# FoX attention moved beside the Strassen pairs of the input projection, with a ring of three weight parts

## The chip, the core and the metric

The kernel runs on one core of a Trainium2 chip. It is one launch for a whole decoder layer. The metric is the device time in microseconds (us), the median of the runs. Engines are named as in the profile: PE (TensorE) multiplies, PEld is its weight load, DVE (VectorE), ACT (ScalarE) and POOL (GpSimd) do the elementwise work, and SP issues DMAs.

## What is computed

One layer for 1024 prompt tokens and 8 x 4 sample tokens together (1056 columns). An input projection feeds three token mixers, GLA, FoX and HGRN2. Their outputs are gated, merged and projected; a SwiGLU block follows.

```python
z = rms_norm(x) @ w_in          # gq gk gv glr gr fq fk fv ff hq hf hi hg ga gb gc
o_a, o_c = gated_linear_scan(...), gated_linear_scan(...)     # GLA and HGRN2, 4 heads each
# FoX on the prompt, 4 heads of 128, in blocks of 128 queries:
c = cumsum(log_sigmoid(ff + bias))
s = q_block @ k.T / sqrt(128) + c[query] - c[key]             # keys up to the query
o_b = softmax(s) @ v
merged = sigmoid(ga) * (o_a @ wa) + sigmoid(gb) * (o_b @ wb) + sigmoid(gc) * (o_c @ wc)
h = x + merged @ w_out
y = rms_norm(h + swiglu(rms_norm(h)))
```

The sample's FoX reads a paged past as well.

## The kernel before

Activations lie as [128 features, 1056 tokens]. For the projections every fp32 operand is split in a rounded part (h) and a rest (l); three products of these stand for one. The rounding is an ACT copy and the rest a DVE subtraction (`split`, L214 and L215).

The stages, in the order of the program:

- **Start** (`norm1` and two jobs): the norm, and the tiles fq 0, fk 0, fv 0 and fq 1 of the projection.
- **Pairs** (`in_pairs`, `pair_run`): 44 more tiles in 22 pairs. A pair is one level of Strassen's scheme: seven products (P1 to P7), each of two column groups of 12 matmuls of 264 columns, 168 matmuls in all. Four banks of PSUM hold the chains X and Z, one or two hold Y; evictions (L1700 on DVE, L1702 on ACT) read a chain while later products go on adding to it. The weights come as two raw tiles of 512 KB (`pair_load`, L1623). Four sums of them (`pair_sums`, L1630 to L1634) and seven splits (`pair_split`) make the seven parts of a pair, which lie in a ring of four tiles of two parts. After product 3 and later ones of a pair the parts of the next are made; the load after next is asked for behind product 6. `post` multiplies a pair by the norm (L568: one tile on DVE, one on POOL), for the gates gr, hq and hg also by their sigmoid (L572, L574), and stores it in `z_dram` (L602).
- **Mixers** (`phase_m`, then `mixer_jobs` and the first jobs of `out_jobs`): 16 gate tiles as plain jobs (L136, 72 matmuls of 352 columns each) and the first branch jobs. Beside them run generators in queues: `bg` with the four heads of FoX on the prompt, `bg3` with two GLA pairs and four HGRN heads, `bgs` with their sample parts, `bg2` with the sample's FoX (started from head 2). `pump` takes one step of each queue, twice per column chunk of a job.
- **Outputs, feed-forward up and down**: the rest of the branch jobs and the output projection, 22 Strassen pairs (`ffn_up`), plain jobs and 8 Strassen pairs with 126 matmuls (`down_pairs`). All pair stages share `pair_run`.

The framework orders each engine's instructions at build time, by program order as priority and by when its own cost estimates call an instruction ready. So PE's order in the trace is near to the program's but not the same. On the chip each engine takes its queue in turn.

`fox_head` (L723) fetches v, q and k and the log-forget row of its head, turns v token-major (L707), sums the row (L1146), and for each of eight query blocks makes the scores in fp32 (L780), subtracts and takes the maximum (L784, and L789 on the diagonal), Exp (L798), normalises (L797, L799, L800), turns the block by four transposes to a bank (L746, copied by L748) and multiplies by v (L759). A block's turning comes two blocks later (DEPTH).

Of the kernel before, what the change touches and what calls it, by code (L numbers as in the profile page):

```python
# [18 lines left out]
NP = 1024  # L19
# [38 lines left out]
PAIRS += [(n, t) for n, c in (("gq", 2), ("gk", 2), ("gv", 4), ("gr", 4), ("hq", 4), ("hf", 4), ("hg", 4), ("hi", 4)) for t in range(c)]  # L58
# [32 lines left out]
class Body:  # L91
# [179 lines left out]
    def run(self):  # L271
# [21 lines left out]
        self.st = [pe.tile([128, 512], F32, name=f"st{i}") for i in range(3)]  # L293
# [5 lines left out]
    def all_jobs(self):  # L299
# [7 lines left out]
        yield Job(None, 0, None, None, run=self.in_pairs, ahead=lambda: self.pair_ahead(lambda n: self.A["winp"][n], len(PAIRS) // 2))  # L307
# [4 lines left out]
    def phase_m(self):  # L312
# [15 lines left out]
        self.bg += [self.fox_head(h) for h in range(4) if ("fv", h) not in TILES[4:]]  # L328
# [221 lines left out]
    def in_pairs(self, job, nxt):  # L550
# [4 lines left out]
        def phase():  # L555
            self.close("s")
            p = self.open("p", "right", reuse_waits="tile")
            self.u = Slots(p, 6, [128, NT], F32, "pu")
            return [(p.tile([128, 1024], F32R, name=f"rh{i}"), p.tile([128, 1024], F32R, name=f"rl{i}")) for i in range(2)]

        def post(n, y):
# [7 lines left out]
            if name in ("gr", "hq", "hg"):  # L569
                g = [self.u.get(), self.u.get()]  # L570
                for i in range(2):
                    self.sig = nc.scalar.activation(g[i], y[i], AF.Sigmoid)  # L572
                for i in range(2):
                    e[i].tensor_tensor(y[i], y[i], g[i], ALU.mult)  # L574
                self.u.put(*g)
            for i in range(2):
                self.keep(*PAIRS[2 * n + i], y[i])
            self.u.put(*y)
# [15 lines left out]
        self.pair_run(nxt, phase, post, hook)  # L594
# [38 lines left out]
    def mixer_jobs(self):  # L633
        for n, h in TILES[4:]:
            yield self.store(n, h, (lambda h=h: self.bg.append(self.fox_head(h))) if n == "fv" else None)
# [85 lines left out]

    def fox_head(self, h):
        nc = self.nc  # L723
        yield from self.room(5)
        vT, q, k = [self.fetch(n, h) for n in ("fv", "fq", "fk")]
        cb = self.u.get()
        nc.sync.dma_start(cb, self.lf_dram[h:h + 1, :].to_broadcast([128, NT]))
        yield
        v, vu = self.tok_major(vT, None)
        self.u.put(vT)  # L730

        self.sums(cb, NP)
        yield
        if h == SAMPLE_WITH:
            self.bg2.append(self.fox_sample())
        yield from self.room(4)
        o = self.u.get()
        psos = {}

        def turned(i, x):  # L740

            for j0 in range(0, i + 1, 4):
                nb = min(4, i + 1 - j0)
                pt = self.pm.get()
                for j in range(nb):
                    nc.tensor.transpose(pt[:, j * 128:(j + 1) * 128], x[:, (j0 + j) * 128:(j0 + j + 1) * 128], self.ident)  # L746
                P = self.hf.get()
                nc.scalar.activation(P[:, :nb * 128], pt[:, :nb * 128], AF.Copy)  # L748
                self.pm.put(pt)
                if j0 + nb == i + 1:  # L750
                    self.u.put(x)
                yield j0, nb, P

        def values(i, j0, nb, P):
            if i % 4 == 0 and j0 == 0:
                psos[0] = self.pm.get()
            pso = psos[0]
            for j in range(nb):
                nc.tensor.matmul(pso[:, (i % 4) * 128:(i % 4 + 1) * 128], v[:, j0 + j, :], P[:, j * 128:(j + 1) * 128],  # L759
                                 start=j0 + j == 0, stop=j0 + j == i)  # L760
            self.hf.put(P)
            if i % 4 == 3 and j0 + nb == i + 1:
                nc.vector.tensor_copy(o[:, (i - 3) * 128:(i + 1) * 128], pso)
                self.pm.put(pso)

        prev = []
        for i in range(8):
            n = (i + 1) * 128
            x = self.u.get()
            cbd = self.sp.tile([128, 128], F32, tag="cbd", name="cbd", bufs=2)  # L770
            nc.gpsimd.tensor_tensor(cbd, cb[:, n - 128:n], self.cmask, ALU.add)
            m = self.sp.tile([128, 4], F32, tag="fm", name="fm", bufs=4)
            init = -3.0e38
            nm = 0
            tp = turned(*prev.pop(0)) if len(prev) == DEPTH else iter(())
            for s0 in range(0, n, 512):
                part = next(tp, None)
                w = min(512, n - s0)
                ps = self.pm.get()
                nc.tensor.matmul(ps[:, :w], q[:, i * 128:(i + 1) * 128], k[:, s0:s0 + w], start=True, stop=True)  # L780
# [13 lines left out]
                if part:  # L794
                    values(i - DEPTH, *part)
            sm = self.sp.tile([128, 4], F32, tag="fs", name="fs", bufs=4)
# [4 lines left out]
            prev.append((i, x))  # L801
            yield
        for i, x in prev:
            for part in list(turned(i, x)):
                values(i, *part)
            if i < 7:
                yield
        nc.sync.dma_start(self.o_dram[4 + h][:, 0:NP], o[:, 0:NP])
        self.u.put(q, k, vu, cb, o)

    def fox_sample(self):
# [1275 lines left out]
```

## Time and profile before

| what | us |
|---|---|
| median of 3 runs | 1998.83 (1998.76 to 2003.77) |
| the profiled execution | 2003.84 |
| its span in the profile | 2002.0 |
| PE busy | 1936.3 |
| DVE busy | 1372.3 |
| ACT busy | 808.6 |
| POOL busy | 456.6 |

The stages lie in the span like this: start to 75, pairs to 534, mixers to about 1090, outputs to 1262, feed-forward up to 1733, down and the end to 2002. Busy time is the time in which an engine had an instruction in flight. The granted clock is the share of PE's full clock; the two levels are 2.4 and 1.2 GHz, so 0.94 over a stretch means that part of it ran at the lower one.

### The profile page before, as it was taken

What the parts mean: (1) busy time and instruction counts of PE and PEld (TensorE: products, weight loads), DVE (VectorE), ACT (ScalarE), POOL (GpSimd) and SP (SyncE); (2) the same over time, 40 slices, a digit from 0 to 9 for tenths busy, and PEclk for the clock granted to TensorE, in tenths of its full rate; (3) what the DMA queues carried; (4) which work ended last, traced back from release to release, by engine and by line L of the source; (5) the groups of instructions that cost most, each with busy time, mean ns of one, the idle gap of its engine ahead of it and who ended that gap; (6) DMA issues with size and microseconds to landing.
All of it is one profiled execution on the core that took longest, in us unless ns stands there. A gap on an engine that the chain in (4) does not pass through costs nothing. (4 is left out here: it accounts for less than half of the span.)

```text
span 2002.0 us, 36377 instructions
## 1 busy us (share of the span) xinstructions
PE 1936.3 (97%) x14590; PEld 1816.3 (91%) x14590; DVE 1372.3 (69%) x2279; ACT 808.6 (40%) x1448; POOL 456.6 (23%) x269
## 2 busy tenths in 40 slices
PE   8899999999989999999999999999999999999997
PEld 6899999999976777787788999999999999999996
DVE  8866577666476767667744555878777777667965
ACT  5433343333244435355343333543333333323435
POOL 5110122211121322112201631133222322111004
PEclk9999999999988989999999999999999999999999
DMA  3343222333434226676775443221222122333212
GB/s 132 108 158 132 99 106 97 107 107 119 135 139 152 96 98 217 213 225 220 231 252 198 160 156 119 75 75 67 101 80 75 65 83 75 133 113 121 84 59 87
DMA packets 88630, 253.65 MB, mean 127 GB/s; under 512 B 13634, under 2 KB 18690, under 8 KB 88450
## 3 DMA queue, kind: packets, MB, share of 16 engines
q1 hardware_dynamic: 86898, 250.02, 36.8%
q8 instruction: 117, 1.92, 0.4%
q10 hardware_dynamic: 1296, 0.67, 0.1%
q14 instruction: 63, 0.52, 0.1%
q0 software_dynamic: 256, 0.52, 0.1%
HBM read 183.80 MB, written 67.37 MB: 125 GB/s over the span
## 5 line engine op out<-in xcount | busy, mean ns | idle before, releaser
L136 PE MATMUL pg<-x,wh 128*128 128x352 f32 x1692 | 434.0, 336 | 11.5 <-DVE ub L629 6.7
L136 PEld LDWEIGHTS pg<-x,wh 128*128 128x128 f32 x1692 | 298.1, 192 | 37.0 <-issue 26.2
L1693 PE MATMUL pg<-x,wh 128*128 128x264 f32 x1632 | 308.6, 285 | 3.4 <-DVE du L1700 2.3
L136 PE MATMUL pg<-x,wl 128*128 128x352 f32 x846 | 280.6, 332 | 0.1
L1693 PE MATMUL pg<-x,rh 128*128 128x264 f32 x1424 | 267.3, 285 | 2.2 <-DVE fu L1700 2.2
L1693 PEld LDWEIGHTS pg<-x,wh 128*128 128x128 f32 x1632 | 253.3, 188 | 5.7 <-DVE du L1700 2.5
L1693 PE MATMUL pg<-x,wl 128*128 128x264 f32 x816 | 231.7, 284 | 2.3 <-DVE wl L215 2.3
L1693 PEld LDWEIGHTS pg<-x,rh 128*128 128x128 f32 x1424 | 221.7, 189 | 2.5 <-DVE fu L1700 2.4
L1693 PE MATMUL pg<-x,rl 128*128 128x264 f32 x712 | 202.8, 285 | 0.0
L136 PEld LDWEIGHTS pg<-x,wl 128*128 128x128 f32 x846 | 162.4, 192 | 4.2 <-issue 3.0
L1693 PEld LDWEIGHTS pg<-x,wl 128*128 128x128 f32 x816 | 153.4, 188 | 2.5 <-DVE wl L215 2.5
L568 POOL TENSOR_TENSOR pu<-pu,r 128x1056 f32<-128x1056 f32 x21 | 59.2, 2818 | 378.6 <-ACT pu L1702 378.6
L1693 PEld LDWEIGHTS pg<-x,rl 128*128 128x128 f32 x712 | 134.6, 189 | 0.0
L214 ACT ACTIVATE wh<-wf 128x512 fp32r<-128x512 f32 (+2 forms) x110 | 68.1, 619 | 158.9 <-PE pg L1693 120.2
L215 DVE TENSOR_TENSOR wl<-wf,wh 128x512 fp32r<-128x512 f32 (+2 forms) x110 | 85.6, 778 | 46.7 <-ACT wh L214 45.2
L1728 POOL TENSOR_TENSOR fu<-fu,r 128x1056 f32<-128x1056 f32 x22 | 67.2, 3057 | 215.9 <-ACT fu L1702 202.7
L107 ACT ACTIVATE wh<-wf 128x1024 fp32r<-128x1024 f32 (+2 forms) x60 | 51.3, 854 | 146.8 <-PE pg L136 105.8
L1630 DVE TENSOR_TENSOR st<-wf 128x512 f32<-128x512 f32 x44 | 87.2, 1982 | 32.8 <-DMA wf<-in_winp 19.0
L1693 PE MATMUL pg<-pr,wh 128*128 128x264 f32 x544 | 103.1, 288 | 3.7 <-ACT pu L1702 3.7
L1700 DVE TENSOR_TENSOR pu<-pu,pg 128x264 f32<-128x264 f32 x132 | 56.4, 428 | 72.2 <-PE pg L1693 71.9
L215 DVE TENSOR_TENSOR rl<-wf,rh 128x512 fp32r<-128x512 f32 x85 | 69.8, 822 | 47.7 <-ACT rh L214 46.8
L214 ACT ACTIVATE rh<-wf 128x512 fp32r<-128x512 f32 x85 | 53.5, 631 | 112.2 <-PE pg L1693 83.7
(519 smaller groups left out, 4594.6 us busy)
## 6 DMA issues: line engine op xcount, KB each, us to landing
z_dram<-pu SPq DMA_DIRECT2D x44, 528.0 KB
wf<-in_winp SPq DMA_DIRECT2D x44, 512.0 KB
wf<-in_wgu SPq DMA_DIRECT2D x44, 512.0 KB
u<-z_dram SPq DMA_DIRECT2D x36, 528.0 KB
ub<-z_dram SPq DMA_DIRECT2D x28, 528.0 KB
wf<-in_win SPq DMA_DIRECT2D x19, 512.0 KB
a_dram<-fu SPq DMA_DIRECT2D x18, 528.0 KB
du<-a_dram SPq DMA_DIRECT2D x14, 528.0 KB
```

Source lines behind the costliest of these rows:

```text
L107: nc.scalar.activation(wh[:, :n], wf[:, :n], AF.Copy)
L136: nc.tensor.matmul(ps[:m, :CW], a[:, k, :], b[:, sl], start=n == 0, stop=n == 3 * job.kt - 1)
L214: nc.scalar.activation(h, x, AF.Copy)
L215: (eng or nc.vector).tensor_tensor(l, x, h.bitcast(F32), ALU.subtract)
L568: e[i].tensor_tensor(y[i], y[i], self.r1, ALU.mult)
L1630: nc.vector.tensor_tensor(s[0], a2[:, x], a2[:, y], ALU.add)
L1693: nc.tensor.matmul(ps, a[:, w], b, start=first and m == 0, stop=m == 3 * K - 1, skip_group_check=not first)
L1700: nc.vector.tensor_tensor(out, out, ps, ALU.add)
L1728: TT = lambda e, o, x, y, op=ALU.mult: e.tensor_tensor(o, x, y, op)
```

## The change

- The prompt's FoX leaves the mixer stage. Its four heads run in `bg` during the pair stage. `pair_run` gets a function `beside`, called after every column group, and `in_pairs` pumps `bg` there; what is left is drained behind the pairs.
- `fox_head` is rewritten in smaller steps with tiles of its own (`fox_open`): one score bank, one bank of transposes, or one value block per step. Query blocks are fetched and outputs stored one by one. The copy of an output leaves DVE for ACT. A block's turning comes one block later.
- To make room, the ring of the input pairs has three tiles instead of four, the pair stage has five buffers instead of six, and the sums of weights share one buffer and are made in place. The pairs get six PSUM banks instead of seven, FoX two.
- The order of sums, splits and loads changes in all three pair stages: part 0 of the next pair after product 2, then 1, 2 and 3, 4, 5, and part 6 after product 0 of its own pair; the next load follows that.
- The gate tiles gr, hq and hg move behind hf and hi. The sample's FoX is queued from the start of the mixer stage.

```diff
+PAIRS += [(n, t) for n, c in (("gq", 2), ("gk", 2), ("gv", 4), ("hf", 4), ("hi", 4), ("gr", 4), ("hq", 4), ("hg", 4)) for t in range(c)]
@@ phase_m
-        self.bg += [self.fox_head(h) for h in range(4) if ("fv", h) not in TILES[4:]]
+        self.bg2.append(self.fox_sample())
@@ in_pairs
         def phase():
             self.close("s")
             p = self.open("p", "right", reuse_waits="tile")
-            self.u = Slots(p, 6, [128, NT], F32, "pu")
-            return [(p.tile([128, 1024], F32R, name=f"rh{i}"), p.tile([128, 1024], F32R, name=f"rl{i}")) for i in range(2)]
+            self.u = Slots(p, 5, [128, NT], F32, "pu")
+            ring = p.tile([128, 1024], F32R, name="rh"), p.tile([128, 1024], F32R, name="rl")
+            self.fox_open(p)
+            self.bg.append(self.fox_head(0))
+            return [ring]
@@ post
                 self.keep(*PAIRS[2 * n + i], y[i])
+                if PAIRS[2 * n + i][0] == "fv":
+                    self.bg.append(self.fox_head(PAIRS[2 * n + i][1]))
@@
-        self.pair_run(nxt, phase, post, hook)
+        self.pair_run(nxt, phase, post, hook, banks=6, beside=lambda: self.pump(self.bg))
+        self.drain(self.bg)
         self.phase_m()
@@ fox_head, new
+        nc.sync.dma_start(vT, self.z_dram["fv", h][:, 0:NP])
+        nc.sync.dma_start(k, self.z_dram["fk", h][:, 0:NP])
+        nc.sync.dma_start(cb, self.lf_dram[h:h + 1, 0:NP].to_broadcast([128, NP]))
...
+        qs = [query(0)]
+        for _ in range(4):
+            yield
+        nc.vector.tensor_tensor_scan(cb, self.one1.to_broadcast([128, NP]), cb, 0.0, ALU.mult, ALU.add)
+        v = self.fa.get()
+        for q in range(2):
...
+            yield
+        def scores(i):
+            n = (i + 1) * 128
+            if i < 7:
+                qs.append(query(i + 1))
...
             for s0 in range(0, n, 512):
...
+                if s0 + 512 < n:
+                    yield
...
             nc.scalar.activation(x[:, :n], x[:, :n], AF.Exp, bias=sm[:, 0:1], scale=1.0 / RT128, accum_out=sm[:, 1:2])
             nc.vector.reciprocal(sm[:, 2:3], sm[:, 1:2])
             nc.vector.tensor_scalar(x[:, :n], x[:, :n], sm[:, 2:3], None, ALU.mult)
...
             yield
+            return x
+        def values(i, x):
+            Ps = []
+            for j0 in range(0, i + 1, 4):
...
+                    nc.tensor.transpose(pt[:, j * 128:(j + 1) * 128], x[:, (j0 + j) * 128:(j0 + j + 1) * 128], self.fident)
+                Ps.append(self.fp.get())
+                nc.scalar.activation(Ps[-1][:, :nb * 128], pt[:, :nb * 128], AF.Copy)
...
                 yield
+            ps, o = self.pm.get(), self.fb.get()
+            for j in range(i + 1):
+                nc.tensor.matmul(ps[:, 0:128], v[:, j * 128:(j + 1) * 128], Ps[j // 4][:, j % 4 * 128:j % 4 * 128 + 128],
+                                 start=j == 0, stop=j == i)
+            nc.scalar.activation(o, ps[:, 0:128], AF.Copy)
...
+            nc.sync.dma_start(self.o_dram[4 + h][:, i * 128:(i + 1) * 128], o)
+            yield
+        prev = None
+        for i in range(8):
+            x = yield from scores(i)
+            if prev:
+                yield from values(*prev)
+            else:
+                yield
+            prev = i, x
+        yield
+        yield from values(*prev)
@@ pair_split
+        if name == "P5":
+            V.tensor_tensor(s, a2[:, x], a2[:, y], ALU.add)
+        elif name == order[min(order.index("P6"), order.index("P3"))]:
+            V.tensor_tensor(s, s, a1[:, x], SUB)
+        if name == "P3":
+            V.tensor_tensor(a1[:, y], a1[:, y], s, SUB)
+        elif name == "P7":
+            V.tensor_tensor(a2[:, x], a1[:, x], a2[:, x], SUB)
@@ pair_run
+    SPLITS = {2: (0,), 3: (1,), 4: (2, 3), 5: (4,), 6: (5,)}
...
-        for n in (4, 5, 6):
+        for n in (4, 5):
             self.pair_split(n)
-        self.pair_load(1)
-        self.banks(7)
+        self.banks(banks)
...
+                    if beside:
+                        beside()
                 has.add(self.READS[name])
+                if k == 0:
+                    self.pair_split(7 * n + 6)
+                    if last:
+                        self.wf.put(*self.raw)
+                    else:
+                        self.pair_load(n + 1)
+                elif not last:
+                    for j in self.SPLITS.get(k, ()):
+                        self.pair_split(7 * (n + 1) + j)
...
-                elif k >= 3:
-                    if k < 5:
-                        self.pair_sums(k == 3)
-                    for j in ((0, 1), (2, 3), (4, 5), (6,))[k - 3]:
-                        self.pair_split(7 * (n + 1) + j)
-                    if k == 6:
-                        self.pair_load(n + 2)
```

## Rows read from the trace of the kernel before

**Rows 1.** The page's table of engines: busy us, share of the span, instructions.

```profile
PE 1936.3 (97%) x14590; PEld 1816.3 (91%) x14590; DVE 1372.3 (69%) x2279; ACT 808.6 (40%) x1448; POOL 456.6 (23%) x269
```

**Rows 2.** Stretches: length, busy PE, PEld, DVE, ACT, POOL, granted clock, DMA share, GB/s.

```profile
75.00:100.00 25.00, 19.02 (x129) 18.40 (x128) 16.86 (x30) 7.97 (x17) 0.83 (x1) 0.86 0.31 109
...
120.00:534.00 414.00, 414.00 (x3406) 413.97 (x3405) 265.19 (x367) 154.23 (x315) 70.63 (x25) 1.00 0.32 112
200.00:400.00 200.00, 200.00 (x1647) 200.00 (x1646) 137.40 (x179) 78.61 (x158) 43.32 (x15) 1.00 0.30 103
534.00:860.00 326.00, 309.58 (x2044) 243.38 (x2044) 214.37 (x580) 141.49 (x276) 67.82 (x69) 0.94 0.46 156
860.00:1000.00 140.00, 136.28 (x1202) 109.31 (x1202) 99.21 (x228) 63.01 (x121) 33.49 (x18) 0.99 0.70 226
...
560.00:580.00 20.00, 14.80 (x83) 11.78 (x82) 14.93 (x49) 8.53 (x21) 9.13 (x10) 0.83 0.37 140
```

**Rows 3.** Waits of PE in 534:860: who waits for whom, total us, times, longest.

```profile
PE pg L136 <- DVE ub L629: 5.2, 1, 5.2
PE pg L746 <- DVE ub L800: 3.5, 2, 2.8
PE pg L780 <- DVE ub L230: 3.1, 1, 3.1
PE pg L746 <- DVE fs L797: 1.8, 2, 1.7
```

**Rows 4.** Timeline of PE: start, us from first start to last end, instructions.

```profile
671.20 0.60 PE L746 MATMUL pg<-c_ident,u 128*128 128x128 f32 x4
671.64 1.02 PE L780 MATMUL pg<-u,u 128*128 128x512 f32 x2
672.50 1.15 PE L759 MATMUL pg<-h,u 128*128 128x128 f32 x8
673.48 0.27 PE L746 MATMUL pg<-c_ident,u 128*128 128x128 f32 x1
```

**Rows 5.** Groups by line, DVE, in the mixer stage: count, busy us, mean ns, idle before.

```profile
L784 DVE CUSTOM_DVE_ANT_0 u<-pg,u 128x512 f32<-128x512 f32 x6 | 4.1, 689 | 3.8 <-PE pg L780 3.5
L789 DVE CUSTOM_DVE_ANT_0 u<-pg,cbd,fm 128x128 f32<-128x128 f32 x14 | 4.9, 348 | 1.1
L799 DVE RECIPROCAL fs<-fs 128x1 f32<-128x1 f32 x32 | 5.0, 156 | 8.7 <-ACT u L798 4.6 <-ACT ub L798 4.0
L1146 DVE TENSOR_TENSOR_SCAN u<-one,u 128x1024 f32<-128x1024 f32 x3 | 8.4, 2785 | 1.0 <-DMA u<-lf_dram 1.0
...
L800 DVE TENSOR_SCALAR ub<-ub,fs 128x128 f32<-128x128 f32 (+7 forms) x17 | 11.6, 685 | 0.2
L800 DVE TENSOR_SCALAR u<-u,fs 128x768 f32<-128x768 f32 (+7 forms) x15 | 8.3, 552 | 0.3
```

**Rows 6.** The same for ACT.

```profile
L748 ACT ACTIVATE h<-pg 128x512 f32<-128x512 f32 (+3 forms) x48 | 22.7, 484 | 38.4 <-PE pg L746 38.2
L798 ACT ACTIVATE ub<-ub,fs 128x128 f32<-128x128 f32 (+7 forms) x17 | 13.0, 764 | 18.8 <-DVE fs L797 18.5 <-issue 0.4
L798 ACT ACTIVATE u<-u,fs 128x768 f32<-128x768 f32 (+7 forms) x15 | 11.7, 783 | 10.9 <-DVE fs L797 10.9
```

**Rows 7.** Timelines of SP, POOL and DVE in a pair: start, us, instructions.

```profile
300.77 7.82 SPq L1623 DMA_DIRECT2D wf<-in_winp  x2
...
310.87 3.25 POOL L568 TENSOR_TENSOR pu<-pu,r 128x1056 f32<-128x1056 f32 x1 [13.09 <-ACT pu L1702]
...
311.95 2.73 DVE L1630 TENSOR_TENSOR st<-wf 128x512 f32<-128x512 f32 x1
314.61 0.68 DVE L215 TENSOR_TENSOR rl<-wf,rh 128x512 fp32r<-128x512 f32 x1
315.81 2.96 DVE L215 TENSOR_TENSOR rl<-st,rh 128x512 fp32r<-128x512 f32 x1
```

**Rows 8.** The chain that ended last: a load alone, start and us.

```profile
1286.81 3.43 DMA wf<-in_wgu
```

More of the change, by code (lines that the diff above doesn't have):

```diff
@@ L292, in run @@
         pe, s = self.open("pe", "right"), self.open("s", "right")
-        self.st = [pe.tile([128, 512], F32, name=f"st{i}") for i in range(3)]
+        self.st = pe.tile([128, 512], F32, name="st")
         self.u = Slots(s, 12, [128, NT], F32, "su")
@@ L719, in tok_sample, with fox_open @@
         self.pm.put(ps)
+    def fox_open(self, p):
+        nc = self.nc
+        self.fa = Slots(p, 5, [128, NP], F32, "fa")
+        self.fp = Slots(p, 3, [128, 512], F32, "fp")
+        self.fb = Slots(p, 6, [128, 128], F32, "fb")
+        self.fs = Slots(p, 4, [128, 8], F32, "fs")
+        self.fident, self.fmask = [p.tile([128, 128], F32, name="f" + n) for n in ("ident", "cmask")]
+        nc.sync.dma_start(self.fident, self.A["ident"])
+        nc.sync.dma_start(self.fmask, self.A["cmask"])
@@ L722, in fox_head @@
     def fox_head(self, h):
         nc = self.nc
[L724 to L764, printed above, removed]
@@ new lines, in fox_head @@
+        nc.vector.tensor_tensor_scan(cb, self.one1.to_broadcast([128, NP]), cb, 0.0, ALU.mult, ALU.add)
+        v = self.fa.get()
+        for q in range(2):
+            ps = self.pm.get()
+            for i in range(4):
+                c = 4 * q + i
+                nc.tensor.transpose(ps[:, i * 128:(i + 1) * 128], vT[:, c * 128:(c + 1) * 128], self.fident)
+            nc.scalar.activation(v[:, 512 * q:512 * q + 512], ps, AF.Copy)
+            self.pm.put(ps)
+            yield
+        self.fa.put(vT)
@@ L1497, in phase_o @@
         self.exts = list(self.ext.free)
-        self.st = [e.tile([128, 512], F32, name=f"st{i}") for i in range(3)]
+        self.st = e.tile([128, 512], F32, name="st")
         self.u = Slots(o, 13, [128, NT], F32, "ou")
@@ L1813, in phase_d @@
         d = self.open("d2", "right", reuse_waits="tile")
-        self.st = [d.tile([128, 384], F32, name=f"dst{i}") for i in range(3)]
+        self.st = d.tile([128, 384], F32, name="dst")
         self.dring = d.tile([128, 1024], F32R, name="drh"), d.tile([128, 1024], F32R, name="drl")
```

88 lines of the change are left out of this document (39 added, 49 removed).

## The prediction

> **What bounds the kernel now.** First the page's table of engines [rows 1]: TensorE (PE) is busy 97% of the span, so only its gaps and its clock can be won, and moving work is no gain by itself. Then the table of stretches [rows 2], of which the reader should take PE's busy time against the length, and the granted clock. In the pair stage (200:400 stands for it) PE is never idle, its clock is 1.00, and 1647 matmuls take 200 us: 121.4 ns each, 20.4 us for the 168 of a pair. DVE has 137.4 us of 200 there (14.0 per pair), ACT 78.6 (8.0). The mixer stage starts at 534. Its first 326 us hold all of the prompt's FoX. There PE is idle for 326 - 309.58 = 16.4 us, and at a mean clock of 0.94 it loses another 0.06 x 326 = 19.6 us against 2.4 GHz, because it works part of the time at 1.2. So 290 us of work at full clock take 326, and 36 us (11%) are lost. In 860:1000 FoX is over while GLA, HGRN, sample and projection go on: 3.7 us idle and 0.01 x 140 = 1.4 by the clock, 3.7%. Then the waits of PE in that first stretch [rows 3]: 3.5 + 1.8 us are FoX's transposes waiting for its softmax on DVE, 3.1 its scores behind a reduction's eviction, and 5.2 a projection held by an eviction that DVE did late. At least half of the 16.4 us has FoX's name. So the question is whether the same FoX work costs less in a stage whose PE has no gaps.
>
> **What FoX costs PE.** The pitch is read from successive starts at full clock [rows 4]: four transposes 671.64 - 671.20 = 0.44 us, a score of 512 columns 672.50 - 671.64 = 0.86, four value blocks (two records each) 673.48 - 672.50 = 0.98. A head has 128 x (1 + ... + 8) = 4608 score columns, which are nine times 512 (7.7 us), 36 + 8 transposes (4.8) and 36 value blocks (8.8): 21.4 us, and 85.6 for four heads. The change removes this from the mixer stage and adds the same to the pairs; the arithmetic is unaltered.
>
> **Part 1, the pairs with FoX beside them.** A head has 40 yields and so takes 41 calls of the pump. There are 14 calls per pair, so a head lasts 2.93 pairs and four take 11.7 of the 22: the drain behind the pairs finds nothing. Where FoX runs a pair becomes 20.4 + 85.6 / 11.7 = 27.7 us of PE. On DVE a head brings [rows 5] 3584 columns off the diagonal at 689 / 512 ns (4.8 us), eight diagonal blocks at 0.348 (2.8), the normalising (11.6 + 8.3) / 4 = 5.0, a scan of 2.8 and sixteen column operations of about 0.156 (2.5): 17.9 us, 6.1 per pair, so DVE has 14.0 + 6.1 = 20.1 of 27.7 us (73%). On ACT [rows 6] a head brings (13.0 + 11.7 + 22.7) / 4 = 11.9 us and some 3 for the copies of v and of the outputs; a pair then has 13.1 of 27.7 us. Neither becomes the bound. The eight mask additions of a head on POOL are small against that engine's 43.3 us of 200.
>
> What can still hold PE is order, since the engines take their queues in turn. A bank of the X chain is written again three groups after the group that ended in it: 3 x 20.4 / 14 = 4.4 us for the eviction without a FoX step, 6 with one between groups. Six banks are what the chains X, Z and Y use at most, so the seventh was no cover; zero, or one eviction (0.43 us) a pair if I am wrong. A block's transposes come three to five pumps behind its scores, at least 6 us. The wait of a transpose for DVE in the mixer stage bounds this: zero below, 5.3 us in all as measured [rows 3] above. I take 5, as DVE is as loaded here as there. **The pairs grow by 85.6 + 5 = 91 us.**
>
> **Part 2, the shorter ring and the later loads.** Sums and splits keep their number (four sums, seven splits a pair); they move from the last four products to nearly one per product, and each is five or six products ahead of its use (14.6 us or more in the pairs). The raw weights of the next pair are now loaded after product 0 and split 6. Before, the second load was issued as late as 7.5 us behind the first (308.6 - 0.33 - 300.77, [rows 7]), when the last split had freed its tile. After: 1.3 us for the split (an ACT copy and a DVE subtraction of some 0.65), 3.4 for one load alone [rows 8], so the first half is there 4.7 us after product 0; it is wanted at 2 x 2.9 = 5.8. Two loads at 3.4 give 8.1, wanted at 8.7. In the down pairs (18 matmuls, 2.2 us a product) 4.7 is 0.3 late, and five products cover it. Zero for all 52 pairs; without that cover it would be 0.3 us for each of 8 pairs, some 2 us. SP carries, per head, three loads of 512 KB, eight queries and eight outputs of 64 KB in place of four loads and one store of the same sum. An output's store waits on SP for ACT's copy, and behind it may stand the raw weights; a group (1.5 us) eats the 1.1 us to spare, though not with FoX's 7.3 us per pair in it. The starts of the three pair stages lose three of the four sums ahead of their first products. At the first of them, in 75:100, PE was idle 25 - 19.02 = 6.0 us [rows 2]; against that FoX's tiles are opened in the room of the closing pool. I take zero and keep half of it, 3 us, either way.
>
> **Part 3, what the mixer stage gives back.** 290 - 85.6 = 204 us of work at full clock is left of its first stretch. At the loss of 860:1000 (3.7%) it takes 212 us and the stage saves 114. At its own present loss (11%) it takes 229 and saves 97. The first is the nearer row in kind (no FoX in it), the second in place (constants, the first GLA chain and its half-clock stretches stay). I take the middle, **105 us**. The sample's attention starts at once instead of beside head 2, so its page loads fall on the stage's first half; the DMA share was 0.46 there and 0.70 in 860:1000, where PE kept 97%.
>
> **Sum.** 91 - 105 = -14 us. The profiled execution took 2003.84 us (span 2002.0), 5.0 above the median of the runs shown, 1998.83; 2003.84 - 14 = 1990, and against the median 1985. Ends: 85.6 - 114 - 3 = -31 and 91 - 97 + 3 = -3, so 1968 to 1996; most of it between 1972 and 1994.
>
> **Rivals.** *The loss moves along.* The mixer stage keeps 11% and the pairs get FoX's waits: 91 - 97 = -6, with 2 us of part 2 against it 1995. For it speaks that the half-clock stretches may be GLA's own; against it that the waits with FoX's name go.
>
> *More than forecast.* Both best ends: 1968. For it: between 120 and 534 PE was busy for all 414 us [rows 2], so no wait of the pair stage has reached it.
>
> *The mixer stage is left bare.* FoX was work that was ready while the six GLA and HGRN chains waited for their own DVE, ACT and POOL steps. If PE then idles as it does in 560:580 (5.2 of 20 us, 26%), 204 us take 276, the stage saves 50, and 91 - 50 = +41 gives 2040. It decides from a stage that saves less than 91 us, that is when over 31 us of its new 235 are lost. Against it: 860:1000 has no FoX and 2.7% idle, and the projections still fill.
>
> *DVE holds PE in the pairs.* If each of the 32 blocks keeps PE for 3.5 / 2 = 1.75 us, the mean wait of a transpose for its normalising [rows 3], the pairs grow by 85.6 + 56 and the sum is +37: 2036. It decides where DVE comes more than the 6 us of distance late. POOL can do that: while its multiplication of 3.25 us runs, a DVE sum takes 2.73, and beside the next multiplication a split's subtraction 2.96, where one of the same size between them takes 0.68 [rows 7]. By the Trainium skill, "SBUF — State Buffer", section "Who interferes with whom", DVE and GpSimd share one port pair, and "Whoever issues first gets the shared pair for the whole instruction"; the rows agree, and by that rule the normalising, moved beside these multiplications, would stand still for up to 3 us, which is this rival. I hold it unlikely, because a pair has such collisions today and PE does not notice.
>
> **How the numbers follow.** Forecast 0.50, the loss moves along 0.20, more 0.13, bare mixers 0.10, DVE in the pairs 0.07. A measurement of this kernel tells 0.3% (6 us) from no change, so the bound of faster is 1993: nearly all of the forecast, all of "more" and a little of the second case make 0.64; slower is the last two, 0.17; 0.19 is left for no change. The range of 0.8 leaves out the slower cases and a tail of the gain: 1966 to 2004.
>
> **What the profile after would show.** No gaps of PE over 1 us in the FoX pairs, 27 to 28 us per FoX pair and 20.4 after them, the mixer stage starting at 534 + 91 = 625 and its pure projection stretch (1092 before) at 1092 - 14 = 1078, no line of fox_head behind the pairs, and the clock of the mixers' first half above 0.94. I am wrong if the mixers' idle share rises, if waits on DVE or POOL stand before pair matmuls, or if a pair waits for its weights.

## The result, and the profile after

The changed kernel takes 2082.52 us (median; its executions range from 2056.97 to 2087.29) against 1999.80 us for the kernel before on the same chip: ratio 1.0379, 95% interval 1.0305 to 1.0453. Forecast were 1985 us and a gain; it is 3.8% slower.

Its profiled execution is the shortest (2056.97 us, span 2055.0). A second profile (e0 below) has a span of 2080.6, near the median. From the first to the last product of each stage's pairs:

| us | before | after | after, second profile |
|---|---|---|---|
| pairs of the input projection | 458.8 | 557.3 | 557.7 |
| mixers and outputs, to the FFN's first pair product | 739.3 | 662.5 | 686.2 |
| the FFN's up pairs | 464.4 | 496.6 | 497.4 |
| behind the up pairs, to the end | 263.9 | 263.9 | 263.4 |

The pairs grow by 98.5 us, the mixers give back 77 or 53, and the FFN's up pairs, in which there is no FoX, lose 32. The page's table of engines after, beside [rows 1]:

```profile
PE 1949.7 (95%) x14590; PEld 1826.0 (89%) x14590; DVE 1351.2 (66%) x2267; ACT 815.7 (40%) x1480; POOL 450.6 (22%) x269
```

The same 14590 matmuls are there, but in a longer span. The stretches after, with the columns of [rows 2]:

```profile
75.00:632.00 557.00, 538.32 (x4255) 520.88 (x4255) 342.21 (x660) 226.07 (x499) 89.53 (x58) 1.00 0.34 114
...
632.00:1295.00 663.00, 632.76 (x4504) 543.74 (x4502) 382.72 (x757) 263.20 (x397) 152.77 (x110) 0.95 0.53 177
632.00:860.00 228.00, 211.38 (x1480) 160.25 (x1479) 127.54 (x305) 80.81 (x150) 47.30 (x37) 0.90 0.58 193
860.00:1000.00 140.00, 133.23 (x1222) 101.19 (x1221) 93.70 (x222) 64.44 (x109) 27.76 (x15) 0.96 0.64 208
1295.00:1791.00 496.00, 465.35 (x3700) 461.69 (x3701) 366.66 (x442) 184.69 (x363) 127.66 (x44) 0.98 0.22 72
```

Two stretches of before that those need for comparison, then the second profile's mixers:

```profile
534.00:1274.00 740.00, 713.91 (x5067) 608.80 (x5066) 461.32 (x1014) 312.53 (x517) 175.18 (x142) 0.97 0.52 174
1274.00:1738.00 464.00, 456.70 (x3701) 455.26 (x3701) 357.17 (x441) 184.63 (x364) 127.43 (x44) 0.99 0.23 77
```

```profile
634.00:1320.00 686.00, 652.22 (x4501) 552.47 (x4499) 384.67 (x757) 262.74 (x397) 153.74 (x110) 0.92 0.52 171
634.00:860.00 226.00, 209.00 (x1300) 151.39 (x1298) 112.63 (x273) 66.48 (x122) 42.30 (x32) 0.80 0.53 173
```

In the mixers PE was idle for 26 us before and is idle for 30 after, in a stage shorter by 77: FoX has gone, but the gaps have stayed. The clock is lower, 0.95 and 0.92 instead of 0.97. In the FFN's up pairs the idle time rises from 7 us to 31, and the time at 1.2 GHz from 10 us to 24, which at half speed is 7 us more: together nearly all of the 32. The waits of PE there, before and after (who waits for whom, total us, times, longest):

```profile
PE pg L1693 <- ACT fu L1702: 2.8, 1, 2.8
PE pg L1693 <- DVE fu L1700: 2.2, 1, 2.2
```

```profile
PE pg L1722 <- ACT fu L1731: 26.8, 11, 2.8
PE pg L1722 <- DVE fu L1729: 2.0, 1, 2.0
```

Both lines are the pairs' evictions, by ACT and by DVE. After, eleven products wait some 2.4 us each for ACT to empty a bank, nearly all of them one in every second pair. One such stall, from the timelines of POOL, DVE, ACT and PE of the kernel after (start, us, instructions, idle time before):

```profile
1504.70 2.85 POOL L1761 TENSOR_TENSOR fu<-fu,r 128x1056 f32<-128x1056 f32 x1 [1.20 <-ACT fu L1806]
1505.14 2.96 DVE L1671 TENSOR_TENSOR st<-wf 128x512 f32<-128x512 f32 x1
1507.63 2.79 POOL L1761 TENSOR_TENSOR fu<-fu,fu 128x1056 f32<-128x1056 f32 x1
1508.13 0.63 ACT L214 ACTIVATE rh<-st 128x512 fp32r<-128x512 f32 x1 [3.23 <-DVE st L1671]
1508.13 2.83 DVE L1677 TENSOR_TENSOR wf<-wf,wf 128x512 f32<-128x512 f32 x1
...
1510.89 0.68 DVE L215 TENSOR_TENSOR rl<-st,rh 128x512 fp32r<-128x512 f32 x1
1511.61 0.69 DVE L1673 TENSOR_TENSOR st<-st,wf 128x512 f32<-128x512 f32 x1
1512.33 0.63 ACT L214 ACTIVATE wh<-st 128x512 fp32r<-128x512 f32 x1 [3.00 <-DVE st L1673]
1512.87 0.37 ACT L1731 ACTIVATE fu<-pg 128x264 f32<-128x264 f32 x1
...
1513.29 0.81 PE L1722 MATMUL pg<-x,wh 128*128 128x264 f32 x2 [2.42 <-ACT fu L1731]
```

Read it backwards. PE waits for an eviction of 0.37 us. The eviction stood in ACT's queue behind the split of the sum for P6 (L214), which waited 3.00 us for the sum (L1673). The sum is made in place, so it had to wait until the split of P5 had read the old content (L215). And DVE was late with all of it, since two of its instructions took 2.96 and 2.83 us beside GpSimd's (POOL's) products; instructions of the same size take 0.68 and 0.69 once POOL is done, as the next two lines show. Ten of the eleven waits come behind such a split. The other rival in ACT's queue, the sigmoids (L1806) that wait for POOL's products, is not new: they wait 26.0 us before and 26.4 after.

### The profile page after: what moved, and what is told of

The parts are those of the page before. It is cut to its first block, busy times and chain, and to the rows that moved or that the text cites. A ratio compares the mean times of both kernels' runs of the same rounds, so it can differ in the third digit from the quotient of the medians.

```text
span 2055.0 us, 36519 instructions
## 1 busy us (share of the span) xinstructions
PE 1949.7 (95%) x14590; PEld 1826.0 (89%) x14590; DVE 1351.2 (66%) x2267; ACT 815.7 (40%) x1480; POOL 450.6 (22%) x269
## 5 line engine op out<-in xcount | busy, mean ns | idle before, releaser
L1722 PE MATMUL pg<-x,wh 128*128 128x264 f32 x1888 | 368.5, 291 | 17.8 <-ACT fu L1731 14.3
L1722 PEld LDWEIGHTS pg<-x,wh 128*128 128x128 f32 x1888 | 296.8, 190 | 26.2 <-ACT fu L1731 15.6
L136 PEld LDWEIGHTS pg<-x,wh 128*128 128x128 f32 x1692 | 297.5, 190 | 23.2 <-issue 17.2
L1722 PE MATMUL pg<-x,wl 128*128 128x264 f32 x944 | 269.6, 286 | 1.7 <-DVE wl L215 1.7
L1722 PE MATMUL pg<-x,rh 128*128 128x264 f32 x1168 | 226.7, 290 | 11.7 <-ACT fu L1731 9.7
L1722 PEld LDWEIGHTS pg<-x,rh 128*128 128x128 f32 x1168 | 183.7, 191 | 15.6 <-ACT fu L1731 10.5
L215 DVE TENSOR_TENSOR wl<-wf,wh 128x512 fp32r<-128x512 f32 (+1 forms) x156 | 134.7, 864 | 75.5 <-ACT wh L214 72.4
L1722 PE MATMUL pg<-x,rl 128*128 128x264 f32 x584 | 167.2, 286 | 0.0
L214 ACT ACTIVATE wh<-wf 128x512 fp32r<-128x512 f32 (+1 forms) x156 | 95.8, 617 | 165.1 <-PE pg L1722 118.9
L1722 PEld LDWEIGHTS pg<-pr,wh 128*128 128x128 f32 x704 | 109.5, 189 | 12.6 <-ACT pu L1731 7.9
L215 DVE TENSOR_TENSOR rl<-wf,rh 128x512 fp32r<-128x512 f32 x87 | 81.1, 934 | 33.8 <-ACT rh L214 32.2
L1722 PE MATMUL pg<-pr,wl 128*128 128x264 f32 x352 | 100.3, 285 | 0.0
L1671 DVE TENSOR_TENSOR st<-wf 128x512 f32<-128x512 f32 x44 | 65.4, 1485 | 45.2 <-DMA wf<-in_winp 35.7
```

Of the source, the lines that this page charges most:

```text
L136: nc.tensor.matmul(ps[:m, :CW], a[:, k, :], b[:, sl], start=n == 0, stop=n == 3 * job.kt - 1)
L214: nc.scalar.activation(h, x, AF.Copy)
L215: (eng or nc.vector).tensor_tensor(l, x, h.bitcast(F32), ALU.subtract)
L1671: V.tensor_tensor(s, a2[:, x], a2[:, y], ALU.add)
L1722: nc.tensor.matmul(ps, a[:, w], b, start=first and m == 0, stop=m == 3 * K - 1, skip_group_check=not first)
```

## The experiments

The runs are called e0 to e17. In the tables "half clock" is the time at 1.2 GHz: over stretches of 1 us, the sum of (1 - granted clock) / 0.5. The expectations count the up stage of the FFN from a later mark, 441 us before and 477 after; here it is 464.4 and 496.6.

### The FFN: the order of sums, splits and loads

e0, a second profile of the changed kernel, with no edit:

> The changed kernel once more, for a second profile. Theory A (the new order of loads, sums and splits costs the time, in every stage that has pairs): the up stage of the FFN again some 36 us longer than the kernel before, with the idle time of TensorE ahead of the ACT evictions of that stage. If this execution's span is near 2080 rather than 2055, the further 25 us should lie in the stage where the granted clock is lower than in the first profile; theory A has it in the FFN, the rival (the FoX steps are what is slow) in the pairs of the input projection.

Measured: 2085.17 us. The FFN lost the same 33 us. The further time of this profile (25.6 us) was in neither of the two places named: 24 us of it are in the mixers, at a clock of 0.80 in the first 226 us.

e1, the new order alone, in the kernel before:

```diff
-        self.st = [e.tile([128, 512], F32, name=f"st{i}") for i in range(3)]
+        self.st = e.tile([128, 512], F32, name="st")
...
-    def pair_sums(self, first):
...
+    SPLITS = {2: (0,), 3: (1,), 4: (2, 3), 5: (4,), 6: (5,)}
...
+                if k == 0:
+                    self.pair_split(7 * n + 6)
...
+                        self.pair_load(n + 1)
```

> The kernel before with the new order of loads, sums and splits in all three pair stages and nothing else of the change: FoX stays in the mixers, the ring stays at four parts. Theory A: slower than the kernel before by at least the 36 us of the FFN's up stage, 2035 to 2065 us. Rival B (the order costs nothing, as the prediction had it, and it is the FoX move that disturbs the clock for the rest of the kernel): 1997 to 2003 us, the up stage back at 441 us.

Measured: 2030.52 us, ratio 1.0143 (1.0113 to 1.0173). The up pairs take 496.5 us, the input pairs 457.1. The order costs the FFN its 32 us, so rival B falls, and the input pairs without FoX nothing. The total is 5 us under theory A's range: 32 instead of 36 in the FFN, and mixers 6 us shorter with 27 us at half clock instead of 48.

e2, the changed kernel with the old order (and its three buffers for sums) in the FFN:

```diff
-        self.pair_run(nxt, phase, post, hook)
+        self.old_pair_run(nxt, phase, post, hook)
...
-            self.pair_run(nxt, phase, None, hook, lambda n
+            self.old_pair_run(nxt, phase, None, hook, lambda n
```

> The changed kernel with the old order (loads behind the last product of a pair, sums in buffers of their own, splits from the fourth product on) in the FFN's up and down pairs alone; the input pairs keep FoX, the ring of three and the new order. Theory A: the up stage goes back from 477 to about 441 us, and the total falls by 36 us or more from the changed kernel's, to 2020 to 2045. Rival B: the up stage stays at 470 to 480 us and the total within 5 us of the changed kernel's.

Measured: 2040.74 us, ratio 1.0179 (1.0147 to 1.0211); the up pairs take 462.8 us. Theory A holds, but 37 us remain that have nothing to do with the FFN.

The two halves of the new order. A buffer for each sum, in the changed kernel's FFN (e3) and in the kernel before with the new places (e4):

```diff
-            V.tensor_tensor(s, s, a1[:, x], SUB)
+            V.tensor_tensor(s1, s, a1[:, x], SUB)
...
-            V.tensor_tensor(a1[:, y], a1[:, y], s, SUB)
+            V.tensor_tensor(s2, a1[:, y], s1, SUB)
```

> The changed kernel with a buffer for each of the three sums in the FFN's pairs (nothing made in place there); the places of loads, sums and splits stay the new ones. Theory A1 (it is the one sum made in place, which waits for the split that reads it, while ACT's split behind it holds the evictions): the up stage falls back to 441 to 448 us, the total by 30 us or more. Theory A2 (it is where the splits and loads stand, so that they come late or meet GpSimd's post-processing): the up stage stays at 470 us or more.

> The kernel before with the new places of loads, sums and splits in all pairs, but a buffer for each of the three sums. If the two halves of the new order (places, and one sum made in place) cost their own shares, as the 19 us that three buffers gave back of the 44 us that the old order gave back say, this is 2012 to 2022 us, between the kernel before and its version with the whole new order (2030). If the sum made in place is all of it: 2000 to 2006. If the places are all of it: 2025 to 2033.

e5, the kernel before with the new `pair_split` and one buffer, but the old places (shown against e1):

```diff
-                if k == 0:
-                    self.pair_split(7 * n + 6)
...
+                if not last:
+                    for j in {3: (0, 1), 4: (2, 3), 5: (4, 5), 6: (6,)}.get(k, ()):
+                        self.pair_split(7 * (n + 1) + j)
+                    if k == 6:
+                        self.pair_load(n + 2)
```

> The kernel before with the old places of splits and loads (load behind the last product, splits from the fourth product on), but the three sums made in place in one buffer, each at its split. Own shares: 2010 to 2022 us. The sum in place is all: 2025 to 2033. The places are all: 2000 to 2006.

| up pairs, us (PE's wait for ACT's evictions) | three sums | one sum in place |
|---|---|---|
| old places (before; e5) | 464.4 (2.8) | 494.6 (24.6) |
| new places (e4; e1) | 477.0 (15.7) | 496.5 (26.4) |

The medians are 2016.42 us for e4 (ratio 1.0082) and 2037.14 for e5 (1.0182), above both ranges that allowed the sum in place a cost; e3 has 2066.01, with 477.8 us for the up pairs, so neither A1 nor A2 holds alone. Neither half is all: the sum in place costs 30 us with the old places, the new places 13 with three sums, and together they cost 32, not 43. Two causes that don't add have a third in common, and the timeline above offers one: POOL.

### GpSimd beside VectorE

e10, the changed kernel with one letter changed in the FFN:

```diff
         def post(n, y):
-            e = V, P
+            e = V, V
```

> The changed kernel with GpSimd's three products per gate of the FFN's up stage given to VectorE (11 x 3 more of 1.25 us there). Theory E (the sums and splits come late because VectorE's instructions beside a GpSimd product take 2.8 to 2.9 us instead of 0.7): TensorE's wait for the ACT evictions in the up stage falls from 26.8 to under 10 us and the stage from 477 to 450 to 460, the total by 17 us or more. Rival F (the chain of splits and one sum is late by its own length, and 41 us more on VectorE make it later): 26 us of wait or more, the total as the changed kernel's (2083) or up to 15 us above.

Measured: 2047.41 us, 35 us under the changed kernel, with 43 products moved (not the 33 that I had counted). The up pairs take 455.3 us, less than in the kernel before. PE's waits in them, and two groups of DVE instructions (count, busy us, mean ns, idle before), first in this run, then in the kernel after:

```profile
PE pg L1722 <- ACT fu L1731: 0.3, 1, 0.3
...
L1671 DVE TENSOR_TENSOR st<-wf 128x512 f32<-128x512 f32 x21 | 14.4, 686 | 2.9 <-DMA wf<-in_wgu 2.9
...
L1677 DVE TENSOR_TENSOR wf<-wf,wf 128x512 f32<-128x512 f32 x21 | 14.4, 687 | 2.3 <-DMA wf<-in_wgu 2.0
```

```profile
L1671 DVE TENSOR_TENSOR st<-wf 128x512 f32<-128x512 f32 x21 | 49.5, 2358 | 9.4 <-DMA wf<-in_wgu 9.4
...
L1677 DVE TENSOR_TENSOR wf<-wf,wf 128x512 f32<-128x512 f32 x21 | 33.8, 1609 | 0.7
...
L1761 POOL TENSOR_TENSOR fu<-fu,r 128x1056 f32<-128x1056 f32 x22 | 67.4, 3065 | 214.8 <-ACT fu L1731 201.6 <-ACT fu L1806 13.2
```

DVE takes over 54 us of products and still is busy for less: 332.5 us in this stage against 366.7. The order of the change is left as it was, so in the FFN it is harmful only beside POOL. The collisions themselves are not new: in the FFN of the kernel before the same sum is nearly as slow, and PE hardly waits (2.8 us, above):

```profile
L1630 DVE TENSOR_TENSOR st<-wf 128x512 f32<-128x512 f32 x21 | 45.6, 2171 | 13.6 <-DMA wf<-in_wgu 13.2
```

The Trainium skill, "SBUF — State Buffer", section "Who interferes with whom", says that a DVE instruction with two SBUF inputs contends with a GpSimd instruction that reads SBUF. These rows agree: 2358 ns on average beside the products, 686 without them.

The same in the kernel before, in the FFN alone (e12) and then behind the input pairs as well (e13):

```diff
-            e = nc.vector, nc.gpsimd
+            e = nc.vector, nc.vector
```

> The kernel before with GpSimd's three products per gate of the FFN's up stage given to VectorE, and nothing else. In the changed kernel this took the stage (first to last product of its pairs) to 455 us, against 464 in the kernel before. Theory E (two engines that slow each other, in the old order too): 455 us here too, 1993 to 1997 in all against 2003.5. Rival F (in the old order the sums stand early enough, and 41 us more of work on VectorE there make it late): 464 us or more, 2003 to 2015.

> The same, and the products behind the pairs of the input projection on VectorE too (21 of 2.9 us on GpSimd become 21 of 1.25 on VectorE, and the products with a sigmoid). Theory E: the pair stage 453 to 457 us instead of 459, the total 1988 to 1996. Rival F: as the run with the FFN's alone, or up to 10 us above.

Measured: 1997.58 us, ratio 0.9966 (0.9949 to 0.9983), up pairs 455.9 us; and 1998.17 us, 0.9978 (0.9958 to 0.9998). Theory E holds in the FFN (the total is 0.6 us above its range): the kernel before hid most of its collisions, not all. In its input pairs there is nothing to win (458.8 us again), against what I expected.

### What FoX costs where

The heads load v and store it; the rest of `fox_head` is left out, in the kernel before (e6) and in the changed one (e7):

```diff
     def fox_head(self, h):
...
-        self.sums(cb, NP)
...
+        nc.sync.dma_start(self.o_dram[4 + h][:, 0:NP], vT[:, 0:NP])
```

> The kernel before without FoX attention on the prompt (its heads only load v and write it out as the result; scores, softmax and products with v are left out). It measures the prediction's third part by itself. As predicted the stage from the last pair to the barrier gives back 105 us: 543 becomes 438, the total 1895 to 1902. If a mixer stage without FoX is held by the other mixers' waits and by a clock that falls between their short instructions: 455 to 485 us for the stage, 1915 to 1945 in all, with 50 us and more at the half clock in the rows.

> The changed kernel with the same left out (its heads load v and write it out as the result). It measures the second part in the pairs of the input projection by itself, with the ring of three. If FoX's own steps are all that lengthens the pairs: 459 to 463 us for the pair stage instead of 557, the mixers and the FFN as in the changed kernel, total 1985 less or more 15. If the ring of three or the new order costs something in these pairs: 475 us and more.

Measured: 1931.09 us and 1988.43 us. The mixers' stretch of e6, and the pairs' of e7:

```profile
534.00:1203.00 669.00, 637.75 (x4503) 548.21 (x4502) 387.18 (x758) 258.50 (x394) 156.73 (x110) 0.94 0.56 182
```

```profile
76.00:544.00 468.00, 455.99 (x3697) 454.10 (x3697) 271.60 (x416) 170.26 (x348) 72.03 (x26) 0.99 0.36 122
```

FoX's absence gives the mixers 70 us, not 105, with 31 us of idle time left and a lower clock. In the pairs FoX costs 557.3 - 468.0 = 89.3 us. But the pairs are 9 us longer than before even without it, between the two ranges expected. PE waits there for evictions behind a sigmoid; from the timeline of ACT, DVE and POOL of the same run:

```profile
371.67 3.27 POOL L571 TENSOR_TENSOR pu<-pu,r 128x1056 f32<-128x1056 f32 x1 [14.69 <-ACT pu L1639]
372.53 2.97 DVE L215 TENSOR_TENSOR wl<-wf,wh 128x512 fp32r<-128x512 f32 x1
...
374.98 1.08 ACT L575 ACTIVATE pu<-pu 128x1056 f32<-128x1056 f32 x1 [2.58 <-POOL pu L571]
...
376.49 0.93 ACT L1639 ACTIVATE pu<-pg 128x264 f32<-128x264 f32 x3
```

Two runs of the kernel without FoX ask whether it is the new order of these gates (e11 has the old one, below, and six buffers) or POOL (e14 has its products on VectorE):

```diff
-                for i in range(2):
-                    g = self.u.get()
...
+                g = [self.u.get(), self.u.get()]
+                for i in range(2):
+                    self.sig = nc.scalar.activation(g[i], y[i], AF.Sigmoid)
```

> The changed kernel without FoX's heads on the prompt (they load v and write it out as the result, as before), with six tiles for pairs instead of five and the old order in the gate pairs behind a pair: both sigmoids, then both products. Its pair stage took 467 us with the new order there, 459 in the kernel before. Theory G (each sigmoid now waits in ACT's queue behind the product of the one before it, and the evictions behind it): the pair stage falls back to 459 to 462 us and the wait for ACT's evictions there from 9.8 to under 5 us. Rival H (the ring of three or the new order of splits): 465 to 468 us, the wait as it was.

> The changed kernel without FoX's heads on the prompt (they load v and write it out as the result), with GpSimd's products in both pair stages on VectorE. Its pair stage took 468 us against 459 in the kernel before, with the old order of gates as with the new. Theory E (the ACT evictions there stand behind a sigmoid that waits 2.6 us for a GpSimd product of 3.3 us, and behind splits that VectorE does in 2.5 to 3.0 us beside it): 456 to 460 us. Rival H (the ring of three parts, one part less ahead): 465 to 468 us.

Measured: 1984.02 and 1983.15 us; 468.3 us for the pairs with the old gates (wait 9.4 us: theory G falls), 454.3 with the products on VectorE (wait 1.9 us: theory E). In five gate pairs a sigmoid waits some 2.4 us for POOL in the kernel before as well:

```profile
293.73 1.09 ACT L572 ACTIVATE pu<-pu 128x1056 f32<-128x1056 f32 x1 [2.39 <-POOL pu L568]
```

There, and in e1, it is done while PE works on the second product of the next pair. In e7 (374.98 above) PE is in the third by then, and the third's second group waits, because it adds to a bank whose eviction stands behind the sigmoid. Why the sigmoid comes later in these pairs, and not in the new order alone (457.1), isn't settled; the ring of three and the order of the pairs, which puts the gates one behind another, were not tried apart.

### The mixers' clock

Idle products, in the kernel of e2 (e8) and in the kernel before (e9):

```diff
+                if h == 0:
+                    self.fill(ps, 6)
                 nc.tensor.matmul(ps[:NS, :NS], l, r, start=True, stop=True)
...
+    def fill(self, ps, n):
+        xh = self.X[0][0]
+        for _ in range(n):
+            self.nc.tensor.matmul(ps[:, 0:CW], xh[:, 0:128], xh[:, 0:CW], start=True, stop=True)
```

> The changed kernel with the old order in the FFN (2040.7 us) and idle products of two resident tiles (352 columns, 0.16 us each, into a bank that the real product then overwrites) ahead of the short products of the sample scans (six each) and of the scans' scores (four each), some 26 us of TensorE if nothing hides them. Theory C (the mixers lose their time to the half clock, which comes after TensorE's waits there): the granted clock of the first 150 us of the mixers stays above 0.95, the total falls by 15 us or more, to 2000 to 2025. Rival D (the clock is low for another reason, or the waits lie on a chain that the products don't shorten): 2040 to 2065.

> The kernel before with the same idle products. It loses about 24 us to the half clock in its mixers and has 26 us of waits there. Theory C: 1985 to 2003 us. Rival D: 2015 to 2030, the products' own time added.

Measured: 2019.48 us, 21 less than e2, and 2022.61 us, 19 more than the kernel before. The mixers of e8:

```profile
634.00:1292.00 658.00, 635.43 (x4659) 556.75 (x4658) 396.10 (x758) 259.93 (x397) 153.99 (x110) 0.98 0.55 179
```

Half clock falls from 130 us to 24 in the changed kernel, and the stage from 695 to 658 although the idle products are added. (e2's profile is of its slowest execution, 2053.54 us; the medians differ by the 21 us.) In the kernel before, with 48 us at half clock, the same products find little to mend (37 us remain) and cost their own time. So theory C holds where FoX has gone, rival D where it has stayed. All profiles in one table, mixers and outputs, us (the runs with idle products are left out, the last column, length - half clock / 2, estimates the stage at 2.4 GHz throughout):

| FoX | kernels | length | half clock | idle | at level clock |
|---|---|---|---|---|---|
| in the mixers | before, e1, e4, e5, e12, e13 | 731 to 746 | 27 to 62 | 26 to 28 | 715 to 719 |
| elsewhere or left out | after, e0, e2, e3, e6, e7, e10, e11, e14, e16 | 663 to 695 | 62 to 130 | 30 to 36 | 628 to 634 |

(e16 is told of below.)

### Both repairs

The changed kernel with the diffs of e10 and e13, with idle products (e15: three and two, e17: six and four) and without (e16):

> The changed kernel with both repairs: GpSimd's products in both pair stages on VectorE, and idle products in the mixers' gaps, half as many as in the run with filled gaps (three ahead of each short product of the sample scans, two ahead of each of the scans' scores, some 13 us of TensorE). If each gives what it gave alone (35 us the first, 10 to 21 us the second): 2022 to 2040 us. By the stages the FoX move itself, at level clock, costs some 10 us, so it should stay above the kernel before, and above its version with the same products on VectorE by 25 us or more; under 2003 would say that this account is wrong.

> The changed kernel with GpSimd's products in both pair stages on VectorE, and no idle products. Stages as the runs before gave them: pairs 541 us, mixers and outputs 663 to 695 by the clock they get, FFN's up stage 456: 2000 to 2030, most likely 2018, that is 15 to 20 us above the kernel before with the same products on VectorE (1998), and what is left to the FoX move of the loss lies in the mixers' clock alone. If under 1995, the FoX move pays once GpSimd is out of the pairs' way.

> The same with idle products in the mixers' gaps as many as in the first run with filled gaps (six and four). If the clock sets it (72 us of half clock with the light fill, 24 with the full one): 1985 to 1997, at or below the light fill's 1998.5 and the kernel before. If the idle products' own time (some 13 us more) eats what the clock gives: 1998 to 2010.

Measured: e15 1998.50 us, ratio 0.9970 (0.9944 to 0.9995); e16 2023.75, 1.0119 (1.0078 to 1.0160); e17 2012.25, 1.0029 (0.9998 to 1.0060). The stretches of pairs and mixers of e16, and below them those of e13, the kernel before with the same products on VectorE:

```profile
76.00:617.00 541.00, 534.61 (x4254) 518.67 (x4253) 350.01 (x686) 229.17 (x499) 19.05 (x39) 1.00 0.35 117
617.00:1301.00 684.00, 648.41 (x4507) 551.41 (x4505) 384.45 (x758) 262.70 (x397) 147.95 (x103) 0.93 0.53 172
```

```profile
75.00:534.00 459.00, 453.02 (x3699) 452.38 (x3698) 287.26 (x442) 172.61 (x347) 2.33 (x7) 0.99 0.34 115
534.00:1268.00 734.00, 707.97 (x5061) 604.55 (x5061) 461.42 (x1015) 311.73 (x517) 169.43 (x135) 0.98 0.54 175
```

Without POOL in the way the pairs with FoX take 541.4 us instead of 557.3. From e13 to e16 they grow by 82.6 us and the mixers give back 51.1; at level clock they would give back 83.6 (99 and 34 us at half clock). At level clock the FoX move comes out at nothing; by the medians it costs 25.6 us (15 to 20 were expected). The clock accounts for 32 between these two profiles, of which e13's is of its fastest execution. The expectation of e15 was a miss, and its "under 2003" came true: the account in it that the move costs 10 us by its work was wrong. I had added up the FFN's repair and the filling, and forgotten that the same repair takes 16 us from the input pairs. It is 0.3% under the kernel before (the interval ends at 0.9995), as the kernel before with the FFN's products on VectorE is, by one changed letter and without idle work. The twelve times of e17 lie in two groups, 1999 to 2006 and 2018 to 2022 us; its profile, of the second, has 72 us at half clock. Its median is 2 us above both expected ranges. So more filling doesn't hold the clock surely.

## Why the prediction was wrong

*Bound and FoX's own cost: right.* 85.6 us of PE work plus 5 were forecast for FoX in the pairs; it is 89.3 beside POOL and 541.4 - 454.3 = 87.1 without. Neither DVE nor ACT became the bound, the drain found nothing (FoX's last instruction ends at 409 us), and no wait by FoX's name exceeds 2 us:

```profile
PE pg L1722 <- ACT pu L1731: 9.5, 6, 2.3
PE pg L818 <- ACT fp L812: 1.9, 2, 1.4
PE pg L818 <- DVE fs L796: 1.7, 1, 1.7
```

*Part 2, with the evictions of part 1: wrong by 41 us.* "Zero for all 52 pairs" failed in the FFN (+32; e1, e2, e10) and in the input pairs (+9; e7, where it is open which part of the change brings it). The step counted the distance from a split to its product, as DMA and PE see it. It didn't count what stands in ACT's queue behind a split or a sigmoid that waits, namely the evictions. Part 1 had given an eviction 4.4 us until its bank is written again, and priced a miss at zero, or 0.43 us a pair. Nine of the eleven waits in the FFN stand at just such a place, the first group of the fifth product, with 2.41 us each, and so do the five of the gate pairs, with 1.4 to 2.3 us. The step also left the sum made in place, which ties DVE to ACT and ACT to DVE, without a price; and it took DVE's 0.65 us for a split although [rows 7] has 2.73 and 2.96 beside POOL. The rival "DVE holds PE in the pairs" had these rows and the first half of this mechanism (POOL makes DVE late), but was priced for FoX's normalising alone, and its chance, 0.07, came from "a pair has such collisions today and PE does not notice". That was true of the old order, in the stage I had looked at.

*Part 3: wrong by 28 to 52 us.* The stage was to give back 105; it gave 77 and 53, and 70 in the kernel before without FoX. At level clock it gives back 82 to 84, which is about FoX's own 85.6. The step that failed is the middle between two loss rates, 11% and 3.7%: it treated idle time and clock as a surcharge on FoX that goes with it. The new first stretch has 16.6 us of idle time and a clock of 0.90, in the second profile 17.0 and 0.80: with 0.10 x 228 = 22.8 and 0.20 x 226 = 45.2 us for the clock, 17% and 28% are lost. The waits of PE in the mixers after, beside [rows 3]:

```profile
PE pg L1313 <- DVE skq L1190: 8.1, 5, 5.2
PE pg L1113 <- POOL h L1100: 5.5, 5, 1.9
...
PE pg L1313 <- issue: 2.1, 1, 2.1
PE pg L1313 <- ACT vn L723: 2.0, 1, 2.0
```

FoX's waits did go, as forecast; those of the sample's scans (L1313) and of the prompt's (L1113) came in their place. FoX had probably been the work that stood in their gaps: PE never waits for `skq` in the kernel before, but for 6.0 us in the same kernel without FoX (e6). The rival "the mixer stage is left bare" named this, with 50 us saved, and got a chance of 0.10. It priced the loss as 26% of idle time; measured are 7 and 8%, and most of the loss is the clock. So the second profile's 53 us meet its 50 partly by luck.

*The sum.* By the second profile: pairs 98.9 - mixers 53.1 + up pairs 33.0 = +79; forecast was 91 - 105 = -14. Two rivals came true in part and at once, in one case outside the stage for which it was priced; as alternatives they had 0.17 together, and neither reached 2082. Of the signs named ahead, the clock of the mixers' first half (0.90 and 0.80, not above 0.94) and the mixers' idle share (from 3.5 to 4.5%) told rightly against the forecast. "Waits on DVE or POOL before pair matmuls" looked at the wrong engine: the waits stand on ACT, with DVE and POOL behind it.

## What to carry to other kernels

Work taken out of this stage gave back about its own time at level clock, and less as measured: before counting the stage's gaps as gain, ask whose they are, and whether the work that leaves was the one that filled them. An order shared by several stages has to be priced in each of them, with the durations that its instructions have beside the other engines' there, and with what stands behind a waiting instruction in its queue. A collision that is hidden today can cost time after the next change of order, so a rival that rests on one deserves more than a few per cent.

## What the runs showed of the hardware that was not expected

Nearly the same waits of the same kernel are followed by stretches at half clock of very different length. Stretches of 3 us of the kernel after, with the columns of [rows 2], in its two profiles:

```profile
655.00:658.00 3.00, 1.48 (x7) 0.98 (x7) 2.40 (x13) 1.09 (x5) 2.39 (x3) 0.73 0.31 66
658.00:661.00 3.00, 1.22 (x5) 1.16 (x6) 1.12 (x4) 2.07 (x8) 0.81 (x2) 0.50 0.86 302
...
673.00:676.00 3.00, 3.00 (x15) 1.95 (x16) 0.73 (x1) 0.31 (x2) 0.00 (x0) 0.50 0.00 0
...
679.00:682.00 3.00, 3.00 (x39) 2.33 (x38) 2.87 (x8) 1.87 (x5) 0.94 (x1) 1.00 0.02 5
```

```profile
670.00:673.00 3.00, 1.67 (x6) 1.17 (x6) 2.88 (x7) 0.27 (x1) 0.00 (x0) 0.74 0.00 0
673.00:676.00 3.00, 3.00 (x15) 1.72 (x14) 0.88 (x3) 0.27 (x1) 0.00 (x0) 0.50 0.00 0
...
715.00:718.00 3.00, 3.00 (x7) 1.75 (x6) 1.05 (x2) 0.19 (x1) 0.00 (x0) 0.50 0.62 170
...
721.00:724.00 3.00, 3.00 (x24) 2.36 (x23) 2.60 (x6) 0.37 (x1) 0.00 (x0) 1.00 0.92 321
```

Both executions have two gaps of PE here, of 1.7 to 2.2 us each. In the first the clock falls at them and is back after some 20 us; in the second it falls for 3 us, recovers, falls again at a third gap (670 to 673) and stays at 1.2 GHz for some 48 us, while PE counts as busy throughout. This stretch and the next one at half clock (14 us in the first, 34 in the second) make up most of the 25.6 us between the two profiled executions. What decides between the two isn't settled; the runs with idle products had less half clock, and no run had it surely.
